# Embedding loads moved ahead of weight loads in a compression stage, and the order of the first weight splits

## The chip, the core and the metric

The kernel runs on one core of one Trainium2 chip. The core has a matrix engine (TensorE, in the profile PE for its matmuls and PEld for its weight loads), a vector engine (DVE), a scalar engine (ACT), GpSimd (POOL) and SyncE (SP). Each engine takes its instructions strictly in program order, and they are synchronised by semaphores. POOL and SP also issue transfers from memory (DMAs). Matrix products are collected in the banks of PSUM, from which ACT and DVE read them.

The metric is the device time of one execution in microseconds (us), and of several executions the median. Less is better.

## The reference

One layer of a decoder: a normalised input `h` goes through one wide projection, whose columns feed sparse attention (with compressed, selected and windowed keys and values), a gated MLP and the merge gates. Then come an output projection, a per-layer embedding and a last normalisation. The sequence has 512 positions, the model 2048 channels. What matters here is the beginning, up to the compression of the keys and values:

```python
h = rms_norm(x, norm_g[l])
proj = h @ w_in[l]
q, kv, g_logits, z_a, uv, z_b, merge_logits = jnp.split(proj, SPLIT_IDX, axis=-1)
k_c, v_c, k_s, v_s, k_w, v_w = [t.reshape(b, s, A_KV_GROUPS, HEAD_DIM)
                                for t in jnp.split(kv, 6, axis=-1)]

def compress(kv, pe, w1, w2):
    b, s, g, d = kv.shape
    ch = kv.reshape(b, s // CMP_STRIDE, CMP_STRIDE, g, d)
    nc = s // CMP_STRIDE - CMP_RATIO + 1
    blocks = jnp.concatenate([ch[:, r:nc + r] for r in range(CMP_RATIO)], axis=2)
    blocks = blocks + pe[None, None, :, None, :]
    hid = jax.nn.silu(jnp.einsum('bnlgd,lde->bnge', blocks, w1))
    return jnp.einsum('bnge,ef->bngf', hid, w2)
```

`compress` is called for keys (`pe_k`, `w1_k`, `w2_k`) and for values (`pe_v`, `w1_v`, `w2_v`). `pe` is the embedding that the title speaks of, 32 x 64 numbers; `w1` and `w2` are the weights.

## The kernel before

**Numbers in two halves.** Matmuls run on 32-bit operands of reduced precision, so each operand is split into a high half (a rounded copy, made by ACT, L99 or L101) and a low half (what the rounding lost, made by DVE, L105 or L107). A product is three matmuls: high by high, and the two mixed ones.

**Jobs, loads and subs.** The projections are a list of jobs, in a generator (`gemm`) that emits matmuls in program order. The first jobs are kc0 and kc1 (the keys to be compressed), then vc0 and vc1 (the values), then the other keys, named k in the profile, and so on. Each covers 128 output columns and all 16 slices of 128 channels (k = 0 to 15). A load brings 8 slices of weights (512 KB) into one of three raw buffers; it is issued on SP's queue (`load_to`, L139). A sub is 4 slices, half a load. Subs 0 to 3 belong to kc0, 4 to 7 to kc1, 8 to 11 to vc0, 12 to 15 to vc1. `split_to(i)` (L144) makes the high halves of all subs up to i + 1 and the low halves of all up to i; when the second sub of a load has its low half, the raw buffer is free and the next load is issued (L171). The halves of kc0 and kc1 are kept in `ob_h` and `ob_l`; later subs go through four `hi` and three `lo` buffers.

**The first two jobs** run in `early()` (L175), in two passes: first the left 256 positions (hf 0) of kc0 and kc1, then the right 256 (hf 1) of both. Every 4 slices `early` calls `split_to`, with `state["ahead"]` added in the first pass. `fill(n)` advances the generator by n steps, a step being one slice, that is three matmuls in these jobs.

**The beginning of the program** (L582 to L662) interleaves them with the input. The four tiles of x (128 positions each) are squared and summed by ACT (`stats`, L603, L604) and scaled by DVE (`scale`, L607, L610). Then PE transposes them (`turn`, L620), and ACT and DVE write them as act_h and act_l (`turned`). Tiles 0 and 1 are handled first, and the first 14 steps of kc0 run between them. Then come 3 steps, `stats` and `scale` of tile 2, 6 steps, `stats` and `scale` of tile 3, and 9 steps; then the transposes of tiles 2 and 3, with the second pass between them. Since ACT and DVE take instructions in order, where a split is emitted decides which work stands ahead of it.

**The compression** (L681 to L718): POOL clears a corner of the tiles `tokk` and `tokv`, and issues ten loads: for k and then for v `w1` (512 KB, L688), and twice in turn `w2` (L692) and the embedding `pe` (L693). `finish("kc1")` (L694) runs the jobs to the end of kc1. Then, for k and v, PE transposes the embedding (L697, into `ps_pe`), and DVE copies it into two places of `tok` (L699, L700). `finish("vc1")` runs vc0 and vc1, and after four more steps `hidden("k")` multiplies `tok` by `w1`. So the transposes stand in PE's order between kc1's last and vc0's first matmul.

Of the kernel before, what the change touches and what calls it, by code (L numbers as in the profile page):

```python
# [20 lines left out]
P = 128  # L21
# [31 lines left out]
def kernel(ctx: ExitStack, tc: tile.TileContext, x, p, norm_g, w_in,  # L53
                      pe_k, w1_k, w2_k, pe_v, w1_v, w2_v, ln_g, ln_b, sgu_w, sgu_b,
                      w_up_a, w_up_b, w_out, w_ple, w_ple_gate, final_g, out):
    nc = tc.nc
    x, out = x[0], out[0]
    p = p[0, 0]
# [10 lines left out]
    def bank(kind, name):  # L69
        return psum.tile([P, 512], F32, tag=kind, name=name)  # L70
# [20 lines left out]
    def flush():  # L91
        todo = list(deferred)
        deferred.clear()
        for f in todo:
            f()

    def high(hi, src, scale=None):
        if scale is None:
            nc.scalar.copy(hi, src)  # L99
        else:  # L100
            nc.scalar.mul(hi, src, scale)  # L101

    def low(hi, lo, src, scale=None):
        if scale is None:
            nc.vector.tensor_tensor(out=lo, in0=src, in1=hi.bitcast(F32), op=ALU.subtract)  # L105
        else:
            nc.vector.scalar_tensor_tensor(out=lo, in0=src, scalar=scale, in1=hi.bitcast(F32),  # L107
                                           op0=ALU.mult, op1=ALU.subtract)
# [10 lines left out]
    jobs, subs, loads = [], [], []  # L119
# [13 lines left out]
    state = {"loads": 0, "high": 0, "low": 0, "ahead": 0, "pops": 2}  # L133
# [7 lines left out]
            raw[state["loads"]] = (t, k0)  # L141
            state["loads"] += 1

    def split_to(i):  # L144
        while state["high"] <= min(i + 1, len(subs) - 1):
            job, k, n, li = subs[state["high"]]
            t, k0 = raw[li]
            if job.keep is not None:
                hi = ob_h[:, job.keep + k // 4].rearrange("p (n c) -> p n c", n=n)
            elif k >= job.kt - job.tail:  # L150
                hi = f_tiles["th"][:, k - job.kt + job.tail:][:, :n]
            else:
                hi = stream.tile([P, n, job.cols], F32R, tag="hi", name="hi", bufs=4)
            src = t[:, k - k0:k - k0 + n]
            high(hi, src)
            parts[state["high"]] = [hi, None, src]
            state["high"] += 1
        while state["low"] <= min(i, len(subs) - 1):
            job, k, n, li = subs[state["low"]]
            pt = parts[state["low"]]  # L160
            if job.keep is not None:
                pt[1] = ob_l[:, job.keep + k // 4].rearrange("p (n c) -> p n c", n=n)
            elif k >= job.kt - job.tail:
                pt[1] = f_tiles["tl"][:, k - job.kt + job.tail:][:, :n]
            else:
                pt[1] = stream.tile([P, n, job.cols], F32R, tag="lo", name="lo")
            low(*pt)
            state["low"] += 1
            li = subs[state["low"] - 1][3]
            if state["low"] == len(subs) or subs[state["low"]][3] != li:  # L170
                load_to(li + 3)  # L171
# [3 lines left out]
    def early():  # L175

        ps = [bank("g", "ps_" + job.name) for job in jobs[:2]]
        for hf in range(2):
            sl = slice(256 * hf, 256 * hf + 256)
            for i, job in enumerate(jobs[:2]):  # L180
                for k in range(job.kt):
                    s = 4 * i + k // 4
                    if k % 4 == 0:
                        flush()
                        split_to(s + state["ahead"] if hf == 0 else 3 + s if i else 7)
                    hi, lo, _ = parts[s]
                    ah, al = job.act(k)
                    st, sp = k == 0, k == job.kt - 1
                    w = k % 4
                    nc.tensor.matmul(ps[i][:, sl], hi[:, w], ah[:, sl], start=st, stop=False)  # L190
                    nc.tensor.matmul(ps[i][:, sl], hi[:, w], al[:, sl], start=False, stop=False)
                    nc.tensor.matmul(ps[i][:, sl], lo[:, w], ah[:, sl], start=False, stop=sp)
                    if not sp:
                        yield
                if hf:
                    flush()
                    job.evac(ps[i])
                    done.add(job.name)
                yield
# [60 lines left out]
    def fill(n):  # L260
        for _ in range(n):
            next(run, None)

    def finish(name):
        while name not in done:
            next(run)
        flush()
# [314 lines left out]
    with tc.tile_pool(name="xin", bufs=4, side="right") as xin:  # L582
        xt = [xin.tile([P, D], F32, tag="xt", name=f"xt{t}") for t in range(TT)]
        g_row = xin.tile([KT, P], F32, name="g_row", bufs=1)
        g_col = xin.tile([P, KT], F32, name="g_col", bufs=1)
        st = xin.tile([P, TT, 2], F32, name="st", bufs=1)
        nc.sync.dma_start(g_row, norm_g.rearrange("(k p) -> k p", p=P))
        for t in range(TT):
            nc.sync.dma_start(xt[t], x[t * P:t * P + P])
            if t == 1:  # L590
                load_to(1)
        load_to(2)

        spin = bank("g", "ps_spin")

        def keep_busy(n):

            for _ in range(n):
                nc.tensor.matmul(spin[:, :P], ident, ident, start=True, stop=True)

        def stats(t):
            sq = xin.tile([P, D], BF16, tag="sq", name="sq", bufs=1)
            nc.scalar.activation(sq, xt[t], AF.Square, accum_out=st[:, t, 0:1])  # L603
            nc.scalar.activation(st[:, t, 1:2], st[:, t, 0:1], AF.Sqrt, bias=eps_t, scale=1.0 / D)  # L604

        def scale(t):
            nc.vector.reciprocal(st[:, t, 0:1], st[:, t, 1:2])  # L607
            for c in range(0, D, D if t % 2 == 0 else D // 2):
                sl = slice(c, c + (D if t % 2 == 0 else D // 2))
                nc.vector.tensor_scalar(out=xt[t][:, sl], in0=xt[t][:, sl], scalar1=st[:, t, 0:1], scalar2=None,  # L610
                                        op0=ALU.mult)

        banks = {}

        def turn(hf, kp):

            b = banks[hf, kp] = bank("ststoo"[len(banks) % 6], "ps_x")
            for j in range(4):
                k, t = 2 * kp + j // 2, 2 * hf + j % 2
                nc.tensor.transpose(b[:, j * P:j * P + P], xt[t][:, k * P:k * P + P], ident)  # L620

        def turned(hf, kp):
            sl = slice(2 * hf * P, 2 * hf * P + 2 * P)
            for j in range(2):
                k = 2 * kp + j
                split(act_h[:, k, sl], act_l[:, k, sl], banks[hf, kp][:, 2 * P * j:2 * P * (j + 1)],
                      g_col[:, k:k + 1], later=True)
            flush()

        keep_busy(10)  # L630
        b = bank("o", "ps_g")
        nc.tensor.transpose(b[:, :KT], g_row, ident[:KT, :KT])
        nc.vector.tensor_copy(g_col, b[:, :KT])
        keep_busy(22)
        for t in range(2):
            stats(t)
            scale(t)
        split_to(0)
        pairs = KT // 2
        for kp in range(4):  # L640
            turn(0, kp)
        for kp in range(pairs):
            turned(0, kp)
            if kp + 4 < pairs:
                turn(0, kp + 4)
            if kp:
                fill(2)
        state["ahead"] = 1
        for t, n in ((2, 3), (3, 6)):
            fill(n)  # L650
            stats(t)
            scale(t)
        fill(9)
        for kp in range(4):
            turn(1, kp)
        for kp in range(pairs):
            turned(1, kp)
            if kp + 4 < pairs:
                turn(1, kp + 4)
            if kp:  # L660
                fill(2)
        state["ahead"] = 2  # L662
# [18 lines left out]
    with tc.tile_pool(name="cmp", bufs=1) as cmp:  # L681
        w1t, w2t, pet = {}, {}, {}
# [2 lines left out]
            nc.gpsimd.memset(tok[n][:, :, :, NCMP:], 0.0)  # L685
        for n, w1, w2, pe in (("k", w1_k, w2_k, pe_k), ("v", w1_v, w2_v, pe_v)):
            w1t[n] = cmp.tile([P, 16, HD], F32, name="w1" + n)
            nc.gpsimd.dma_start(w1t[n], w1.rearrange("l d e -> (l d) e").rearrange("(m p) e -> p m e", p=P))  # L688
            w2t[n] = cmp.tile([HD, 2, HD], F32, name="w2" + n)
            pet[n] = cmp.tile([NCMP, 2, HD], F32, name="pe" + n)  # L690
            for i in range(2):
                nc.gpsimd.dma_start(w2t[n][:, i], w2)  # L692
                nc.gpsimd.dma_start(pet[n][:, i], pe)  # L693
        finish("kc1")  # L694
        for n in "kv":
            b = bank("t", "ps_pe")
            nc.tensor.transpose(b[:, :NCMP], pet[n].rearrange("l i d -> l (i d)"), ident[:NCMP, :NCMP])  # L697
# [236 lines left out]
    n = len(slots)  # L934
# [142 lines left out]
    for cg in range(4):  # L1077
# [10 lines left out]
        for j in range(4):  # L1088
# [4 lines left out]
            h, l = x2_act(k)  # L1093
# [31 lines left out]
```

## Time and profile before

| | us |
|---|---|
| median of 3 runs | 1671.33 |
| lowest and highest run | 1670.41, 1671.61 |
| profiled execution, its own time | 1672.25 |
| span of its trace | 1670.5 |
| PE busy in the span | 1648.9 |
| ACT busy, DVE busy | 617.9, 736.9 |
| POOL busy | 107.8 |
| mean granted clock of TensorE | 0.996 |

The profile is one execution, seen by the hardware profiler. A row of its timeline reads: start, duration, engine, line of the kernel, operation, output and inputs, their shapes, count, and in brackets how long the engine had stood idle and what it waited for. A matmul's duration contains its fill and drain; matmuls overlap, so that the distance between two starts is what one costs. The granted clock is 1 at full speed.

### The profile page before, as it was taken

Reading aid. Unit: us, or ns where it says so; the run is one execution under the profiler, and the core shown is the slowest. Engines: PE = TensorE matmul, PEld = TensorE weight load, DVE = VectorE, ACT = ScalarE, POOL = GpSimd, SP = SyncE. Lnnn points to the kernel's source line nnn. Section 1 sums busy time; section 2 is a strip of 40 time slices with the busy share of each in tenths; the row PEclk is TensorE's granted clock in tenths of the full one; section 3 lists DMA queues with packets and bytes.
Section 4 is the critical chain, followed back from the end, with each engine's and each line's share of the span. In section 5 each row is a group of like instructions: output and inputs, shape, how many; then the busy total and the mean of one; then the engine's idle time right before and its main releaser. Section 6 shows DMA issues by size and latency. Waiting matters only on the chain.

```text
span 1670.5 us, 20864 instructions
## 1 busy us (share of the span) xinstructions
PE 1648.9 (99%) x7981; PEld 1381.6 (83%) x7981; DVE 736.9 (44%) x1487; ACT 617.9 (37%) x1253; POOL 107.8 (6%) x136
## 2 busy tenths in 40 slices
PE   8899999999999999999999999999999999999997
PEld 8779888888888888888888888888888888888886
DVE  6243378988873352343222222332235333333335
ACT  7232356766653322332222222222224222223334
POOL 1000001110110011000000000000000000001100
PEclk9999999999999999999999999999999999999999
DMA  5322421112234333344333333333334433333333
GB/s 191 102 63 79 114 59 52 51 39 51 51 98 117 101 88 89 89 101 113 95 95 101 96 94 101 89 100 101 91 99 155 139 98 88 91 124 91 99 101 126
DMA packets 214482, 159.64 MB, mean 96 GB/s; under 512 B 4832, under 2 KB 190320, under 8 KB 212848
## 3 DMA queue, kind: packets, MB, share of 16 engines
q1 hardware_dynamic: 212976, 151.41, 32.5%
q0 software_dynamic: 1408, 6.92, 1.2%
q8 instruction: 62, 1.02, 0.3%
q14 instruction: 36, 0.29, 0.1%
HBM read 154.12 MB, written 4.19 MB: 95 GB/s over the span
## 4 chain that ended last, share of the span: by engine, by line
PE 93%; DVE 2%; ACT 1%; DMA 0%; issue 0%; DVEq 0%; ACTq 0%
PE ps_wo L230 3%; PE ps_wo L232 3%; PE ps_wo L231 3%; PE ps_mb L223 3%; PE ps_ma L224 3%; PE ps_mb L224 3%; PE ps_ma L223 3%; PE ps_ma L222 3%; PE ps_mb L222 3%; PE ps_pg L231 3%; PE ps_pg L232 3%; PE ps_pg L230 3%; PE ps_za L222 2%; PE ps_t L822 2%; PE ps_za L224 2%; PE ps_za L223 2%
## 5 line engine op out<-in xcount | busy, mean ns | idle before, releaser
L105 DVE TENSOR_TENSOR lo<-raw,hi 128x512 fp32r<-128x512 f32 (+1 forms) x528 | 361.7, 688 | 652.7 <-PE ps_mb L224 127.4
L99 ACT CAST hi<-raw 128x512 fp32r<-128x512 f32 (+1 forms) x528 | 323.5, 615 | 731.6 <-PE ps_wo L232 102.5
L230 PE MATMUL ps_wo<-hi,act_h 128*128 128x512 f32 x256 | 101.0, 395 | 0.0
L232 PE MATMUL ps_wo<-hi,act_l 128*128 128x512 f32 x256 | 99.9, 390 | 0.0
L231 PE MATMUL ps_wo<-lo,act_h 128*128 128x512 f32 x256 | 99.8, 390 | 0.0
L224 PE MATMUL ps_ma<-act_h,lo 128*128 128x512 f32 x256 | 99.7, 389 | 0.0
L223 PE MATMUL ps_mb<-act_l,hi 128*128 128x512 f32 x256 | 99.7, 389 | 0.0
L223 PE MATMUL ps_ma<-act_l,hi 128*128 128x512 f32 x256 | 99.7, 389 | 0.0
L222 PE MATMUL ps_ma<-act_h,hi 128*128 128x512 f32 x256 | 99.7, 389 | 0.0
L224 PE MATMUL ps_mb<-act_h,lo 128*128 128x512 f32 x256 | 99.7, 389 | 0.0
L222 PE MATMUL ps_mb<-act_h,hi 128*128 128x512 f32 x256 | 99.7, 389 | 0.0
L783 ACT ACTIVATE prob<-prob,st 128x512 f32<-128x512 f32 (+3 forms) x128 | 70.7, 555 | 4.2 <-DVE st L774 4.1
L99 ACT CAST pth<-ps_t 128x512 fp32r<-128x512 f32 (+1 forms) x88 | 47.9, 544 | 65.6 <-PE ps_t L822 65.2
L105 DVE TENSOR_TENSOR ptl<-ps_t,pth 128x512 fp32r<-128x512 f32 (+1 forms) x88 | 56.3, 640 | 21.1 <-ACT pth L99 20.2
L774 DVE CUSTOM_DVE_ANT_0 prob<-ps_s,b 128x512 f32<-128x512 f32 (+3 forms) x128 | 56.3, 487 | 9.8 <-PE ps_s L771 9.6
L465 POOL TENSOR_TENSOR m<-sig,sig 128x512 f32<-128x512 f32 x16 | 27.1, 1693 | 493.6 <-DVE sig L463 493.6
L232 PEld LDWEIGHTS ps_wo<-hi,act_l 128*128 128x128 f32 x256 | 48.1, 188 | 10.3
L222 PEld LDWEIGHTS ps_mb<-act_h,hi 128*128 128x128 f32 x256 | 48.1, 188 | 10.0
L223 PEld LDWEIGHTS ps_ma<-act_l,hi 128*128 128x128 f32 x256 | 48.1, 188 | 10.0
L222 PEld LDWEIGHTS ps_ma<-act_h,hi 128*128 128x128 f32 x256 | 48.1, 188 | 10.0
L223 PEld LDWEIGHTS ps_mb<-act_l,hi 128*128 128x128 f32 x256 | 48.1, 188 | 10.0
L224 PEld LDWEIGHTS ps_ma<-act_h,lo 128*128 128x128 f32 x256 | 48.1, 188 | 9.9
(314 smaller groups left out, 3726.8 us busy)
## 6 DMA issues: line engine op xcount, KB each, us to landing
raw<-in_w_in_dram SPq DMA_DIRECT2D x164, 512.0 KB, 3.7
raw<-in_w_out_dram SPq DMA_DIRECT2D x32, 512.0 KB, 3.6
raw<-in_w_ple_gate_dram SPq DMA_DIRECT2D x32, 512.0 KB, 3.6
raw<-in_w_up_a_dram SPq DMA_DIRECT2D x16, 512.0 KB, 3.7
raw<-in_w_up_b_dram SPq DMA_DIRECT2D x16, 512.0 KB, 3.8
xt<-in_x_dram SPq DMA_DIRECT2D x4, 1024.0 KB, 7.7
m<-in_x_dram POOLq DMA_DIRECT2D x4, 1024.0 KB, 8.0
out_dram<-m SPq DMA_DIRECT2D x3, 1024.0 KB, 3.8
```

The lines of the kernel that those rows point to most:

```text
L99: nc.scalar.copy(hi, src)
L105: nc.vector.tensor_tensor(out=lo, in0=src, in1=hi.bitcast(F32), op=ALU.subtract)
L222: nc.tensor.matmul(ps, hi[:, j], ah, start=st, stop=False)
L223: nc.tensor.matmul(ps, hi[:, j], al, start=False, stop=False)
L224: nc.tensor.matmul(ps, lo[:, j], ah, start=False, stop=sp)
L230: nc.tensor.matmul(o, ah[:, sl], hi[:, j], start=st, stop=False)
L231: nc.tensor.matmul(o, ah[:, sl], lo[:, j], start=False, stop=False)
L232: nc.tensor.matmul(o, al[:, sl], hi[:, j], start=False, stop=sp)
L465: nc.gpsimd.tensor_tensor(out=merge_tiles["m"][:, f], in0=merge_tiles[0], in1=t, op=ALU.add)
L774: nc.vector.tensor_tensor_reduce(out=pt[:, j * n:j * n + n], in0=o[:, j], in1=b0[:, 512 - n:], scale=-SLOPE[h], scalar=3.0e38, op0=ALU.add ...
L783: nc.scalar.activation(sl, sl, AF.Exp, bias=st[:, 0, j, hh:hh + 1], scale=-1.0, accum_out=st[:, 1, j, hh:hh + 1])
L822: nc.tensor.transpose(b[:, (2 * e + hh) * P:(2 * e + hh + 1) * P], pts[hh][:, c:c + P], ident)
```

## The change

Three things are edited.

The first is in the compression. For each of k and v both copies of the embedding are loaded ahead of `w1`, and `w2` after it. So POOL's order of loads becomes pe, pe, w1, w2, w2 for k and then the same for v. The tiles are allocated as before.

The second is where the embeddings are transposed: `finish("vc0")` stands in place of `finish("kc1")`, so that the transposes and their copies come in program order between vc0 and vc1.

The third is in the beginning. `split_to` gets a second argument, `more`: the number of subs by which the high halves run ahead of the low ones (1 before, and when it is not given). After the first 14 steps the subs 4 and 5 are split, then `stats` and `scale` of tile 2 follow, then subs 6 and 7, then `stats` and `scale` of tile 3, and only then 18 steps at once. `early` no longer adds `state["ahead"]`, and at sub 7 makes no high half ahead. So the high half of sub 8 is made at the first step of the second pass, and that of sub 9 within kc1's second pass.

```diff
-    def split_to(i):
-        while state["high"] <= min(i + 1, len(subs) - 1):
+    def split_to(i, more=1):
+        while state["high"] <= min(i + more, len(subs) - 1):
...
                     if k % 4 == 0:
                         flush()
-                        split_to(s + state["ahead"] if hf == 0 else 3 + s if i else 7)
+                        split_to(s if hf == 0 else 3 + s if i else 7, 0 if s == 7 else 1)
...
-        state["ahead"] = 1
-        for t, n in ((2, 3), (3, 6)):
-            fill(n)
-            stats(t)
-            scale(t)
-        fill(9)
+        split_to(5, 0)
+        stats(2)
+        scale(2)
+        split_to(7, 0)
+        stats(3)
+        scale(3)
+        fill(18)
         for kp in range(4):
             turn(1, kp)
...
             w1t[n] = cmp.tile([P, 16, HD], F32, name="w1" + n)
-            nc.gpsimd.dma_start(w1t[n], w1.rearrange("l d e -> (l d) e").rearrange("(m p) e -> p m e", p=P))
             w2t[n] = cmp.tile([HD, 2, HD], F32, name="w2" + n)
             pet[n] = cmp.tile([NCMP, 2, HD], F32, name="pe" + n)
             for i in range(2):
+                nc.gpsimd.dma_start(pet[n][:, i], pe)
+            nc.gpsimd.dma_start(w1t[n], w1.rearrange("l d e -> (l d) e").rearrange("(m p) e -> p m e", p=P))
+            for i in range(2):
                 nc.gpsimd.dma_start(w2t[n][:, i], w2)
-                nc.gpsimd.dma_start(pet[n][:, i], pe)
-        finish("kc1")
+        finish("vc0")
```

## The prediction

> **What bounds the kernel now.** I read the page first. TensorE (PE) is busy for all but 21.6 us of the span, so only time in which it waits, or runs at a lower clock, can be won. The two rows of tenths cut the span in 40 slices: PE has gaps in the first two and in the last, and no slice has a granted clock below nine tenths on average. All numbers are microseconds of this one profiled execution.
>
> ```profile
> span 1670.5 us, 20864 instructions
> PE 1648.9 (99%) x7981; PEld 1381.6 (83%) x7981; DVE 736.9 (44%) x1487; ACT 617.9 (37%) x1253; POOL 107.8 (6%) x136
> ...
> PE   8899999999999999999999999999999999999997
> ...
> PEclk9999999999999999999999999999999999999999
> ```
>
> The list of PE's waits over the whole span says which ones are left. Each row is the waiting group, what it waited for, the total, the number of times and the longest.
>
> ```profile
> PE ps_pe L697 <- DMA pev<-in_cmp_pe_v_dram: 3.8, 1, 3.8
> PE ps_kc L192 <- DVE ob_l L105: 2.1, 3, 1.2
> ```
>
> The first is one wait: the transpose of v's embedding (L697), placed after job kc1, waits for the embedding's load. The second is PE in the first two jobs waiting for the low half of a weight split. The timeline of PE (start, duration) shows what surrounds the first.
>
> ```profile
> 45.20 0.28 PE L190 MATMUL ps_kc<-act_h,ob_h 128*128 128x256 f32 x1
> ...
> 45.44 0.28 PE L192 MATMUL ps_kc<-act_h,ob_l 128*128 128x256 f32 x1
> 46.11 0.21 PE L697 MATMUL ps_pe<-ident,pek 32*128 32x32 f32 x1 [0.39 <-PE ps_kc L192]
> 50.17 0.31 PE L697 MATMUL ps_pe<-ident,pev 32*128 32x32 f32 x1 [3.85 <-DMA pev<-in_cmp_pe_v_dram]
> 50.41 0.80 PE L222 MATMUL ps_vc<-act_h,hi 128*128 128x512 f32 x1
> ...
> 55.70 0.53 PE L222 MATMUL ps_vc<-act_h,hi 128*128 128x512 f32 x1
> 56.06 0.39 PE L223 MATMUL ps_vc<-act_l,hi 128*128 128x512 f32 x1
> ...
> 64.02 0.39 PE L222 MATMUL ps_vc<-act_h,hi 128*128 128x512 f32 x1
> ```
>
> Job kc1 issues its last matmul at 45.44 and vc0 its first at 50.41. The 14th of vc0's 48 matmuls starts at 56.06, the first of vc1 (the 49th) at 64.02: (64.02 - 56.06) / 35 = 0.227 a matmul at full speed. The 13 before 56.06 took 5.65, or 0.43 each. The table of stretches (PE, PEld, DVE, ACT and POOL busy, then the granted clock) gives the reason: a clock of 0.50 after the wait.
>
> ```profile
> 50.17:55.70 5.53, 5.53 (x14) 4.31 (x15) 0.35 (x2) 0.19 (x1) 0.00 (x0) 0.50 0.01 3
> ```
>
> So the late load costs twice, the wait and then half speed.
>
> **Part 1, the embeddings: what goes.** POOL issues the ten loads of the compression one after another.
>
> ```profile
> 38.62 0.16 POOL L685 MEMSET tokk<- 128x64 f32 x1 [35.07 <-DVE act_l L107]
> ...
> 39.19 1.34 POOL L688 DMA_DIRECT2D w1k<-in_cmp_w_k_dram  x1 [0.33 <-issue]
> ...
> 44.32 0.52 POOL L693 DMA_DIRECT2D pev<-in_cmp_pe_v_dram  x1
> ...
> 45.96 0.50 POOL L693 DMA_DIRECT2D pev<-in_cmp_pe_v_dram  x1
> ```
>
> v's second embedding copy is the tenth, issued at 45.96, after PE wanted it. The same ten loads remain. In the new order it is seventh: before it stand w1k (1.34) and five small ones, 0.52 each by the rows here, 3.9 in all. It is issued at 39.19 + 3.9 = 43.1, or earlier by what the queue itself starts earlier: the queue waits for the last act_l. The transposes move behind vc0, which by the sum below ends about 54.8.
>
> ```profile
> w1v<-in_cmp_w_v_dram POOLq DMA_DIRECT2D x1, 512.0 KB, 6.8
> ...
> pev<-in_cmp_pe_v_dram POOLq DMA_DIRECT2D x2, 8.0 KB, 4.8
> ```
>
> From issue to landing these loads take 4.8, the slowest on this queue 6.8. So pev lands between 47.9 and 49.9, 4.9 to 6.9 before it is wanted. The wait is gone, and PE goes from kc1 straight to vc0. vc0's splits are ready: they are made while kc1's second half runs (part 2). What the wait cost: kc1's next slot was 45.44 + 0.12 = 45.56. At 0.227, vc0 would have had to start at 56.06 - 13 x 0.227 = 53.10 to be where it was. Difference **7.54**: 4.85 of wait (with the two transposes) and 2.69 of half clock.
>
> The clock's part is the less certain. The row has 5.5 at half clock. The Trainium skill (TensorE: Matmul & The Clock Gate, Part 1, the HAM clock gate) says that a window of about 3.4 us without activity halves the clock and a busy window of the same length, at a free-running phase, restores it. An estimate from that page is 3.4 at half speed and 1.7 lost, against the row's 2.69; by it part 1 would be 6.5 instead of 7.5, varying from run to run. The trace agrees that the drop follows a stretch with hardly a matmul (45.7 to 50.2).
>
> **What comes in its place.** Two transposes and four small DVE copies between vc0 and vc1. Nearest rows for the transposes: eight others between matmuls of 512 columns; for the copies, one of the four before.
>
> ```profile
> 50.59 0.17 DVE L699 COPY tokv<-ps_pe 64x16 f32<-64x16 f32 x1 [2.82 <-PE ps_pe L697]
> ...
> 500.06 0.40 PE L232 MATMUL ps_vn<-hi,act_l 128*128 128x512 f32 x1
> 500.30 1.04 PE L991 MATMUL ps_w<-ident,ws 128*128 128x128 f32 x8
> 501.09 0.48 PE L230 MATMUL ps_vn<-hi,act_h 128*128 128x512 f32 x1
> 501.40 0.39 PE L231 MATMUL ps_vn<-lo,act_h 128*128 128x512 f32 x1
> ```
>
> From the free slot (500.06 + 0.23) to where the stream is back in step (501.40 - 0.23): 0.88 for eight, 0.22 for two. Upper bound: if the 0.55 between 45.56 and 46.11 was the switch itself and not k's load, 0.55 + 0.24 + 0.1 = 0.9. I take **0.3**, near the lower row, since pek's second copy was also landing about 46. The copies lie on DVE ahead of vc1's third split, which PE wants after two splits of twelve matmuls, 5.4 later; uncovered they would cost 4 x 0.17 = 0.7.
>
> **Part 2, the first jobs' splits.** ACT before (L99 makes high halves, L603 the squares), DVE (L105 low halves, L610 the scaling), SP's queue and PE, in order of time:
>
> ```profile
> 19.52 1.25 ACT L99 CAST ob_h<-raw 128x512 fp32r<-128x512 f32 x2
> ...
> 21.36 0.62 ACT L99 CAST ob_h<-raw 128x512 fp32r<-128x512 f32 x1 [0.59 <-DMA raw<-in_w_in_dram]
> ...
> 21.87 0.37 SPq L139 DMA_DIRECT2D raw<-in_w_in_dram  x1
> 21.89 1.91 ACT L603 ACTIVATE sq<-xt 128x2048 bf16<-128x2048 f32 x1
> ...
> 24.62 1.91 ACT L603 ACTIVATE sq<-xt 128x2048 bf16<-128x2048 f32 x1
> ...
> 25.64 0.68 DVE L105 TENSOR_TENSOR ob_l<-raw,ob_h 128x512 fp32r<-128x512 f32 x1
> ...
> 26.04 0.28 PE L190 MATMUL ps_kc<-act_h,ob_h 128*128 128x256 f32 x1
> ...
> 26.86 1.13 ACT L99 CAST hi<-raw 128x512 fp32r<-128x512 f32 x2
> ...
> 27.18 1.42 DVE L610 TENSOR_SCALAR xt<-xt,st 128x1024 f32<-128x1024 f32 x2
> 28.51 0.69 DVE L105 TENSOR_TENSOR ob_l<-raw,ob_h 128x512 fp32r<-128x512 f32 x1
> ...
> 29.25 0.39 PE L192 MATMUL ps_kc<-act_h,ob_l 128*128 128x256 f32 x1 [1.18 <-DVE ob_l L105]
> ...
> 30.56 2.78 PE L620 MATMUL ps_x<-ident,xt 128*128 128x128 f32 x24
> 31.19 5.94 ACT L101 ACTIVATE act_h<-ps_x,g_col 128x256 fp32r<-128x256 f32 x16 [3.21 <-PE ps_x L620]
> 32.06 6.36 DVE L107 SCALAR_TENSOR_TENSOR act_l<-ps_x,g_col,act_h 128x256 fp32r<-128x256 f32 x16 [2.26 <-PE ps_x L620]
> ```
>
> Low half 7 stands on DVE behind the scaling of the fourth x tile and comes at 28.51; PE wants it before 28 and waits 1.18. The new order on ACT is highs 4, 5, squares of tile 2, highs 6, 7, squares of tile 3. High 6 no longer makes the squares wait: they start at 19.52 + 1.25 = 20.8 instead of 21.89, highs 6 and 7 run at about 23.0 to 24.1, and the squares of tile 3 at 24.0 instead of 24.62. On DVE the scaling of tile 2 ends at about 24.5, lows 6 and 7 at 25.1 and 25.8, and the scaling of tile 3 at 28.6 - 0.6 = 28.0. Both low halves are there before PE wants them (26.3 and 27.7). The eight steps of kc1 from 26.04 then last 8 x 0.36 = 2.88 (a step is three matmuls, 45.44 + 0.12 - 45.20 = 0.36), and PE reaches its transposes at 28.92 instead of 30.56: **1.64** gained. They want tile 3 at about 29.0, 1.0 after it is scaled: that is late next, and nothing is paid unless ACT slips by more. The gain lies between 0.6 (tile 3 later by all of that) and 1.64.
>
> High 8 moves between the fourth and fifth of the sixteen act_h. ACT is then 0.6 later for the other twelve. DVE, which starts 0.87 after ACT and is slower (6.36 against 5.94), takes most of that up; PE wants the last low half at (45.20 - 15 x 0.36 + 0.12) - 0.37 = 39.55 before the shift, and DVE ended at 38.42: 1.1 of cover against at most 0.6. High 8's raw tile was issued at 21.87 and used at 26.86 before without a wait, so at 31 it doesn't wait; queued behind it are the act_h, and PE behind these. Highs 9 and 10 and lows 8 to 10 come under kc1's second half, 16 x 0.36 = 5.8 long; they take about 1.3 on ACT and 2.1 on DVE. The load that low 7 releases on SP's queue goes out 2.8 earlier, the one behind low 9 about 1 earlier; none of the raw loads is wanted sooner than 10 after issue there. Cost taken: 0; uncovered at most 0.6.
>
> **Sum.** 7.54 + 1.64 - 0.3 = 8.9 faster. The profiled execution took 1672.25 (its span and 1.75 around it): 1663.4. It lies 0.92 above the median of the three runs, 1671.33, from which the sum gives 1662.4. I forecast 1662.9, between the two, since the half-clock stretch, which I price from this execution, may have been shorter in the faster runs. PE is saturated behind 64 up to the last 10 us, so nothing later takes it back.
>
> **Rivals.** *The reorder gives nothing* (R1): ACT's chain slips and PE waits for tile 3 or for an act_l behind high 8 instead. For it, ACT's and DVE's rows leave hardly a gap there; against it, the slack of 1.0 and the removed 0.59 wait. Gain 7.2: 1664.6. *The half clock comes anyway* (R2), because something other than the wait lowers it. For it: the two are seen together only once. Against it: a second such stretch would show as a slice under nine tenths only if it were longer, but PE has no other wait of its length. Gain 6.2: 1665.6. *The wait only moves* (R3, the slower side): pev's landing, now behind w1k's 512 KB, comes after vc0. It begins to cost from 54.8; with the half clock of 2.69 behind it, it decides from a wait of 6.2, a landing at 61.0, 18 after issue. At 63 the time would be 1673. Against it stands every landing on that queue, 6.8 at most. Where the transposes wait in step with w1k only, there is no loss at all.
>
> **How the numbers follow.** Forecast 0.79, R1 0.10, R2 0.06, R3 0.03, and 0.02 for a late pev that takes back most of the gain. About 0.2%, 3.3 us, is what a measurement of this kernel can tell from no change, so the forecast, R1 and R2 are all faster: 0.95; same 0.02; slower 0.03. The range goes from 1661.0 (the lowest run shown, 1670.41, less 9.2, with the transposes free, rounded down) to 1666.5 (R2 at the profile's own time, 1666.1, and the transposes at their upper bound in part).
>
> **What would show it.** Right: no row of PE waiting for pev; a clock of 1.0 from 40 to 60; vc0's first matmul at about 43.9 and vc1's at 55.2; L697 between them with under 1 us; L192's waits down from 2.1 to about 0.9 (the longest goes); transposes L620 at about 28.9. Wrong: a wait of L620 for xt, of L190 or L191 for act_h or act_l around 33, of L697 for a load, or any stretch under full clock.

## The result and the profile after

The changed kernel takes 1663.42 us (median of 5 runs, 1663.36 to 1663.46), the kernel before 1671.33 (median of 5, 1670.41 to 1671.61). The ratio is 0.9954, with a 95% interval from 0.9939 to 0.9968. That is 7.9 faster, beyond the 0.2% that a measurement can tell from no change, and within the range that was forecast; the forecast was 1662.9. The profiled execution took 1663.46 with a span of 1661.8, so the spans differ by 8.7, against 8.9 in the sum.

From the page of the changed kernel, the same rows as before:

```profile
span 1661.8 us, 20864 instructions
PE 1645.4 (99%) x7981; PEld 1378.3 (83%) x7981; DVE 737.4 (44%) x1487; ACT 617.8 (37%) x1253; POOL 107.7 (6%) x136
...
PE   9999999999999999999999999999999999999997
...
PEclk9999999999999999999999999999999999999999
```

The same number of instructions runs on every engine. The first two slices of PE have gone from 8 to 9, and PE is busy 3.5 less in sum, although its work is the same; the half speed, which made 2.7 of it, is gone. Its list of waits over the whole span, where pev stood first:

```profile
PE ps_spin L599 <- POOL eps_t L75: 1.4, 1, 1.4
PE ps_x L620 <- DVE xt L610: 1.4, 1, 1.4
PE ps_t L824 <- DVE ptl L105: 1.2, 1, 1.2
PE ps_kc L192 <- DVE ob_l L105: 1.0, 2, 0.5
```

No embedding is in it any more (the transposes are now L699), and L192 waits twice instead of three times. The waits for `ps_spin`, `ps_x` and `ps_t` were there before too. PE's timeline around the old place and the new one:

```profile
43.80 0.28 PE L192 MATMUL ps_kc<-act_h,ob_l 128*128 128x256 f32 x1
43.92 0.40 PE L222 MATMUL ps_vc<-act_h,hi 128*128 128x512 f32 x1
...
54.60 0.39 PE L224 MATMUL ps_vc<-act_h,lo 128*128 128x512 f32 x1
54.92 0.24 PE L699 MATMUL ps_pe<-ident,pek 32*128 32x32 f32 x1
55.00 0.22 PE L699 MATMUL ps_pe<-ident,pev 32*128 32x32 f32 x1
55.15 0.50 PE L222 MATMUL ps_vc<-act_h,hi 128*128 128x512 f32 x1
55.49 0.39 PE L223 MATMUL ps_vc<-act_l,hi 128*128 128x512 f32 x1
```

vc0 starts 0.12 after kc1's last matmul, and vc1 at 55.15 instead of 64.02. The stretch that ran at half clock before, in the table of stretches (columns as before), now has 1.00:

```profile
50.17:55.70 5.53, 5.53 (x26) 4.33 (x25) 0.86 (x2) 1.29 (x3) 0.00 (x0) 1.00 0.36 105
```

POOL's timeline, with the new order of loads:

```profile
37.40 0.16 POOL L686 MEMSET tokk<- 128x64 f32 x1 [33.84 <-DVE act_l L107]
...
37.97 1.21 POOL L692 DMA_DIRECT2D pek<-in_cmp_pe_k_dram  x2 [0.33 <-issue]
39.16 1.22 POOL L693 DMA_DIRECT2D w1k<-in_cmp_w_k_dram  x1
...
41.40 1.03 POOL L692 DMA_DIRECT2D pev<-in_cmp_pe_v_dram  x2
```

pev's second copy goes out at 41.9, and the list of DMA issues gives the time from issue to landing:

```profile
pev<-in_cmp_pe_v_dram POOLq DMA_DIRECT2D x2, 8.0 KB, 5.1
```

So it is there at 47.0, eight before PE wants it. And the beginning of the program, on ACT, DVE and PE in order of time:

```profile
20.55 2.03 ACT L603 ACTIVATE sq<-xt 128x2048 bf16<-128x2048 f32 x1
...
22.91 1.13 ACT L99 CAST ob_h<-raw 128x512 fp32r<-128x512 f32 x2
23.95 1.90 ACT L603 ACTIVATE sq<-xt 128x2048 bf16<-128x2048 f32 x1
24.44 1.29 DVE L105 TENSOR_TENSOR ob_l<-raw,ob_h 128x512 fp32r<-128x512 f32 x2
...
26.50 1.42 DVE L610 TENSOR_SCALAR xt<-xt,st 128x1024 f32<-128x1024 f32 x2
...
28.92 2.78 PE L620 MATMUL ps_x<-ident,xt 128*128 128x128 f32 x24
...
31.00 0.64 ACT L99 CAST hi<-raw 128x512 fp32r<-128x512 f32 x1
...
32.41 4.79 DVE L107 SCALAR_TENSOR_TENSOR act_l<-ps_x,g_col,act_h 128x256 fp32r<-128x256 f32 x12 [0.32 <-ACT act_h L101]
```

Low halves 6 and 7 are done at 24.44 + 1.29 = 25.7, tile 3 is scaled at 27.9, and PE's transposes start at 28.92. High half 8 stands at 31.00 among the act_h and makes DVE wait 0.32, of which nothing reaches PE.

### The profile page after: what moved, and what is told of

Read it like the earlier page. It is cut to its first block, busy times and chain, and to the rows that moved or that the text cites. A ratio compares the mean times of both kernels' runs of the same rounds, so it can differ in the third digit from the quotient of the medians.

```text
span 1661.8 us, 20864 instructions
## 1 busy us (share of the span) xinstructions
PE 1645.4 (99%) x7981; PEld 1378.3 (83%) x7981; DVE 737.4 (44%) x1487; ACT 617.8 (37%) x1253; POOL 107.7 (6%) x136
## 4 chain that ended last, share of the span: by engine, by line
PE 95%; DVE 3%; ACT 1%; DMA 0%; issue 0%; SPq 0%; DVEq 0%; ACTq 0%
PE ps_wo L230 4%; PE ps_wo L232 4%; PE ps_wo L231 4%; PE ps_ma L223 3%; PE ps_mb L223 3%; PE ps_mb L222 3%; PE ps_ma L222 3%; PE ps_mb L224 3%; PE ps_ma L224 3%; PE ps_pg L230 3%; PE ps_pg L231 3%; PE ps_pg L232 3%; PE ps_za L222 2%; PE ps_za L224 2%; PE ps_t L824 2%; PE ps_za L223 2%
## 5 line engine op out<-in xcount | busy, mean ns | idle before, releaser
L224 PEld LDWEIGHTS ps_mb<-act_h,lo 128*128 128x128 f32 x256 | 48.0, 188 | 10.0
```

The costliest lines, as they stand in the source:

```text
L224: nc.tensor.matmul(ps, lo[:, j], ah, start=False, stop=sp)
```

## The experiments

The theory at this point: the place of the transposes removes the wait and the half clock; the order of the loads does nothing further; the splits add their 1.6 only because the wait is gone. Rivals: the order of the loads is what counts, or the two parts simply add, or the half clock has nothing to do with the wait. The kernel before was timed beside every group of runs; its medians there were 1670.74 (21 runs, the first four experiments), 1671.63 (15, beside the kernels with 36 matmuls in the wait and with low halves two and four steps earlier) and 1670.76 (21, beside the other three). Its single runs fall into two groups: 27 of the 57 lie at 1670.2 to 1671.0 (median 1670.65), the other 30 at 1671.2 to 1672.4 (median 1671.69). The mean granted clock is 0.997 in 23 of the first and 0.996 in all of the second.

### The embeddings alone

```diff
-        finish("kc1")
+        finish("vc0")
```

together with the new order of loads; the splits stay as before.

> Only the two edits to the embeddings: loads first, transposes behind vc0; the splits are as before. If the parts add up (my theory): PE goes from kc1 to vc0 without a wait, clock 1.0 throughout; vc0's first matmul at 45.6 (kc1's end of before); the low-half waits of L192 stay at 2.1 in sum. Time 1663.42 + 1.64 = 1665.1, and runs as close together as the changed kernel's (0.1), since no half-clock stretch is left. Rival, the splits are what frees vc0: a wait at vc0's first matmul stays, 1666 or more.

Measured: 1664.97 (1664.76 to 1665.24); ratio to before 0.9964 (0.9950 to 0.9978). PE's timeline:

```profile
45.33 0.28 PE L192 MATMUL ps_kc<-act_h,ob_l 128*128 128x256 f32 x1
45.45 0.40 PE L222 MATMUL ps_vc<-act_h,hi 128*128 128x512 f32 x1
```

PE goes straight on at the old end of kc1, at full speed. The theory's number was 1665.1. The runs spread 0.5, somewhat more than expected.

### The splits alone

The edits to `split_to`, `early` and the beginning; loads and place as before.

> Only the edits to the first splits; the embeddings load and are transposed as before. Theory: PE reaches the transposes 1.64 earlier, but the wait for pev ends when POOL's queue delivers it, and that starts only 1.2 earlier (37.4 instead of 38.6 in the two traces). So the wait grows by 0.4 to about 4.2, the half clock behind it stays, and the gain is about 1.2: 1670.1. Rival, the parts add: 1.64, 1669.7. The times can hardly tell these two apart (before's runs spread over 1.2); the trace can: second L697 at 48.9 to 49.0 (theory) or 48.5 (rival).

Measured: 1670.38 (1669.62 to 1670.96); ratio 0.9995 (0.9986 to 1.0004), no difference that can be told. PE's timeline:

```profile
44.78 0.22 PE L698 MATMUL ps_pe<-ident,pek 32*128 32x32 f32 x1 [0.73 <-DMA pek<-in_cmp_pe_k_dram]
48.69 0.24 PE L698 MATMUL ps_pe<-ident,pev 32*128 32x32 f32 x1 [3.70 <-DMA pev<-in_cmp_pe_v_dram]
48.87 0.80 PE L222 MATMUL ps_vc<-act_h,hi 128*128 128x512 f32 x1
```

L192's long wait is gone as in the changed kernel, and PE arrives early at the transposes, only to wait for k's embedding too (0.73). Both waits end when the loads land: pev at 48.7, between the two numbers expected, 1.5 earlier than before, mostly because POOL began 1.25 earlier. So in this execution vc0 starts at 48.87 instead of 50.41, and nearly all of the 1.64 gets through the wait. The median can't show it: its interval reaches from 2.3 faster to 0.7 slower, and the half clock differs from run to run (by the granted clock it lasted from 48.8 to 52.2 here, from 49.2 to 56.0 in the profiled execution of before). With the embeddings moved, the same edit is worth 1664.97 - 1663.42 = 1.55.

### The old order of loads in the changed kernel

```diff
-                nc.gpsimd.dma_start(pet[n][:, i], pe)
-            nc.gpsimd.dma_start(w1t[n], ...)
-            for i in range(2):
+            nc.gpsimd.dma_start(w1t[n], ...)
+            for i in range(2):
                 nc.gpsimd.dma_start(w2t[n][:, i], w2)
+                nc.gpsimd.dma_start(pet[n][:, i], pe)
```

> The changed kernel with the loads in the order of before (w1, then w2 and pe in turns); the transposes stay behind vc0. Theory: pev's last copy is issued at about 44.7 and lands by 50, PE wants it at 54.9, so the place alone removes the wait and the order of the loads is worth nothing: 1663.4, within 0.2, no L697 wait. Rival, the order of the loads is needed: a wait at L697 and up to 1667.

Measured: 1663.50 (1663.41 to 1663.60), the changed kernel's time. POOL's timeline shows pev's second copy as the last load, at 44.38:

```profile
44.38 0.50 POOL L694 DMA_DIRECT2D pev<-in_cmp_pe_v_dram  x1
```

and PE's shows its transpose in its place, without a wait:

```profile
55.04 0.22 PE L698 MATMUL ps_pe<-ident,pev 32*128 32x32 f32 x1
```

The order of the loads, which the change's name puts first, is worth nothing once the transposes stand behind vc0.

### The old place in the changed kernel

```diff
-        finish("vc0")
+        finish("kc1")
```

> The changed kernel with the transposes back between kc1 and vc0; the loads stay in the new order. Theory: pev's last copy is issued at 41.9 and lands at about 47.0, PE wants it at 44.2: a wait of about 2.8 to 3.1. That is shorter than the 4.5 idle of before. If the clock falls only after an idle stretch longer than about 3.4 (the Trainium skill, TensorE: Matmul & The Clock Gate, Part 1), it stays at 1.0 and the time is 1663.4 + 3.0 - 0.3 = 1666.2. If any wait of that kind halves it, up to 2.7 more: 1667 to 1669, with runs that spread.

Measured: 1668.00 (11 runs, 1666.22 to 1669.42); ratio to before 0.9983 (0.9975 to 0.9992). So the order of loads and the splits without the move bring 2.7; against the splits alone (1670.38) the order is worth 2.4 in the old place. PE's timeline:

```profile
43.84 0.28 PE L192 MATMUL ps_kc<-act_h,ob_l 128*128 128x256 f32 x1
44.05 0.24 PE L699 MATMUL ps_pe<-ident,pek 32*128 32x32 f32 x1
47.05 0.21 PE L699 MATMUL ps_pe<-ident,pev 32*128 32x32 f32 x1 [2.76 <-DMA pev<-in_cmp_pe_v_dram]
47.20 0.59 PE L222 MATMUL ps_vc<-act_h,hi 128*128 128x512 f32 x1
47.59 0.63 PE L223 MATMUL ps_vc<-act_l,hi 128*128 128x512 f32 x1
...
50.57 0.54 PE L224 MATMUL ps_vc<-act_h,lo 128*128 128x512 f32 x1
```

The wait was as expected (2.76), the clock not: matmuls of 0.63 follow it up to 50.6. The runs lie in three groups: one at 1666.2 (the time expected with a full clock), six at 1667.85 to 1668.0 and four at 1669.0 to 1669.4. The mean granted clock is 0.998 in the first and 0.996 or 0.997 in the ten others. So a wait of 2.8 halves the clock in nearly every run, for a stretch that differs from run to run.

### The wait filled with work

The kernel before, with matmuls of the identity in the place where PE waits (their result is not used):

```diff
         finish("kc1")
+        wb = bank("o", "ps_warm")
+        for _ in range(36):
+            nc.tensor.matmul(wb[:, :P], ident, ident, start=True, stop=True)
```

> The kernel before, with 36 matmuls of the identity (128 columns, result unused) between kc1's last matmul and the transposes, where PE waits for pev; nothing else is changed. It leaves the wait as it is and fills it with activity. Theory (the half clock comes from the idle stretch alone): second L697 still at about 50.2, clock 1.0 from 40 to 60, no matmul of 0.63 behind it, and 1663.42 + (4.85 - 0.3) + 1.64 = 1669.6 with runs within 0.3 of each other, where before's 21 runs lie between 1670.3 and 1672.2. Rival (the half clock comes anyway, R2 of the prediction): the stretch at 0.50 stays, 1670.7, and the runs spread as before's.

Measured: 1672.87 (1672.68 to 1673.35), slower than either theory had it. PE's timeline gives the reason:

```profile
45.17 8.20 PE L697 MATMUL ps_warm<-ident 128*128 128x128 f32 x72
53.30 0.24 PE L700 MATMUL ps_pe<-ident,pek 32*128 32x32 f32 x1
```

Each of the 36 ran as two, and together they outlasted the wait by some 3. In the table of stretches the clock nevertheless was full:

```profile
40.00:60.00 20.00, 20.00 (x147) 18.74 (x146) 4.93 (x12) 3.51 (x8) 5.48 (x10) 1.00 0.41 103
```

That speaks for the theory, but the time was mis-sized, so it was repeated with 18.

> The kernel before with 18 matmuls of the identity in the wait instead of 36. In the run with 36 each ran as two of 0.114, 8.1 in all, and outlasted the wait; 18 take 4.1 and end at about 49.7, before pev lands at about 50. Theory (the half clock comes from the idle stretch): clock 1.0 from 40 to 60, vc0's first matmul at 50.3, time 1663.42 + 4.55 + 1.64 = 1669.6 (or 1672.87 of the run with 36, less the 3.2 by which its matmuls outlasted pev's landing: 1669.7), runs within 0.3. Rival (the half clock comes anyway): 1671 to 1672, spread over 1 or more.

Measured: 1669.50 (1668.95 to 1670.08). PE's timeline:

```profile
45.24 4.18 PE L697 MATMUL ps_warm<-ident 128*128 128x128 f32 x36
...
49.92 0.24 PE L700 MATMUL ps_pe<-ident,pev 32*128 32x32 f32 x1 [0.32 <-DMA pev<-in_cmp_pe_v_dram]
50.09 0.50 PE L222 MATMUL ps_vc<-act_h,hi 128*128 128x512 f32 x1
50.42 0.40 PE L223 MATMUL ps_vc<-act_l,hi 128*128 128x512 f32 x1
```

pev lands about as late as before and vc0 starts about as late, but at full speed (0.40 instead of 0.63). The time is the theory's 1669.6. The runs spread over 1.1 and not 0.3, though the mean granted clock is 0.998 in all eleven; what spreads them isn't shown. The half clock comes from the idle stretch, and what it costs in the median is 1670.76 - 1669.50 = 1.3, half of the 2.69 in the one execution that the prediction was made from.

With 10, some 2 of idle time are left:

> The same with 10: 2.3 of activity from 45.5 to 47.8, then idle until pev lands at 50, 2.2. Theory A (the clock falls when a stretch near the page's window of 3.4 passes almost idle; 3.0 was enough in the kernel with the old place): 2.2 is too short, clock 1.0, 1669.6 as with 18. Theory B (any stall of two or more halves it): a stretch at 0.50 behind it and 1670.3 to 1672, runs spread.

Measured: 1670.59, in two groups: four runs at 1668.95 to 1669.53, seven at 1670.52 to 1670.80, with a mean granted clock of 0.998 in the first and 0.997 in the second. The profiled one (1670.8) is of the second:

```profile
49.86 0.24 PE L700 MATMUL ps_pe<-ident,pev 32*128 32x32 f32 x1 [1.97 <-DMA pev<-in_cmp_pe_v_dram]
50.04 0.50 PE L222 MATMUL ps_vc<-act_h,hi 128*128 128x512 f32 x1
```

The table of stretches has the clock before and after its fall:

```profile
48.03:51.44 3.41, 1.58 (x7) 1.32 (x8) 0.67 (x4) 0.00 (x0) 0.00 (x0) 1.00 0.06 16
51.44:54.86 3.42, 3.42 (x10) 2.63 (x9) 0.46 (x1) 0.62 (x1) 0.00 (x0) 0.50 0.00 0
```

Theory A falls for most runs: an idle stretch of 2.0 was enough. And the clock fell only at about 51.4, when PE had been at work again for 1.4, and came back 3.4 later. In the traces of the splits alone and of the old place it came back 3.4 after its fall as well (48.8 to 52.2, 47.5 to 50.9). In before's it took twice that:

```profile
49.15:52.57 3.42, 2.40 (x6) 1.95 (x7) 0.35 (x2) 0.00 (x0) 0.00 (x0) 0.50 0.02 5
52.57:55.98 3.41, 3.41 (x9) 2.64 (x9) 0.04 (x1) 0.47 (x1) 0.00 (x0) 0.50 0.00 0
```

There the clock fell while PE still waited, and the first 3.4 at half clock had PE busy for 2.4 only. All this fits a decision taken every 3.4 over the stretch that went before, which some runs meet and some don't; the decision itself is in no trace.

### The two waits that are left in the beginning

In the changed kernel L192 still waits 1.0 for low halves 2 and 3. Two kernels emit them earlier, so that on DVE they stand ahead of act_l that they stood behind: by two steps

```diff
+                    elif k % 4 == 2 and hf == 0 and s < 3:
+                        split_to(s + 1, 0)
```

> The changed kernel, with low halves 1 to 3 of kc0 emitted two steps earlier, so that on DVE each stands ahead of two act_l that it stood behind. Theory: the two waits of L192 that are left (0.47 and 0.48, at 19.7 and 21.9) go, PE reaches the transposes L620 at 28.2 instead of 28.9, and tile 3 is scaled at 27.9, just before: 1663.4 - 0.7 = 1662.7. Rival (DVE is the bound there, so that the act_l come later by what the low halves come earlier): L191 waits instead, 1663.4 or up to 0.5 above.

and by four.

```diff
-                        split_to(s if hf == 0 else ...
+                        split_to(min(s + 1, 3) if hf == 0 and i == 0 else s if hf == 0 else ...
```

> As the kernel with low halves two steps earlier, but four steps earlier. DVE's total work up to low half 5 is the same. Theory: the end of kc0's first pass is set by the last act_l, so there is no more to gain than with two steps: 1662.7, within 0.2. Rival: the earlier high halves make ACT wait for raw tiles or delay act_h, 1663.4 or more.

Two steps: 1662.61 (1662.61 to 1662.74), 0.8 under the changed kernel; one of the two waits goes, one stays:

```profile
PE ps_kc L194 <- DVE ob_l L105: 0.5, 1, 0.5
```

Four steps: 1663.64 (1663.49 to 1663.85), nothing gained. The edit also moved the high halves, and ACT's timeline shows that one of them was emitted ahead of its load:

```profile
19.31 0.62 ACT L99 CAST ob_h<-raw 128x512 fp32r<-128x512 f32 x1 [1.08 <-DMA raw<-in_w_in_dram]
```

So the low halves alone were moved by four steps:

```diff
-                        ... 0 if s == 7 else 1)
+                        ... 0 if s == 7 or (hf == 0 and i == 0 and s) else 1)
```

> The kernel with low halves four steps earlier, but with the high halves left where the changed kernel has them, so that ACT doesn't wait for the raw tile of high half 4 (1.08 in that run). Theory (that wait was the loss): no wait of ACT for raw at 19, L191 waits at most 0.2, 1662.4 to 1662.7. Rival (four steps are too early whatever the high halves do, since act_l comes late): 1663.4 or more.

Measured: 1662.61 (1662.54 to 1662.65). PE's timeline:

```profile
20.64 0.39 PE L191 MATMUL ps_kc<-act_l,ob_h 128*128 128x256 f32 x1 [0.38 <-DVE act_l L107]
...
28.02 2.78 PE L620 MATMUL ps_x<-ident,xt 128*128 128x128 f32 x24
```

PE no longer waits for a low half, but for an act_l (0.38, more than expected), and reaches the transposes at 28.02, about as with two steps (28.09). Both kernels, at 1662.61, beat the kernel before and the changed one, and gain the same. The raw tile that ACT waited for was what the other lost by: without that wait the same low halves are 1.0 faster.

## Why the prediction was right, and where it was off

**The wait is gone, and the transposes cost little: right.** vc0's first matmul was forecast for 43.9 and vc1's for 55.2; they came at 43.92 and 55.15. The detour of the two transposes is 55.49 - 0.23 - (54.60 + 0.23) = 0.43, against 0.3 taken and bounds of 0.2 and 0.9.

**Why it is gone: half right.** The prediction credited the new order of loads and the new place together. With the splits in, the place alone does it (1663.50 with the old loads), and the order alone, in the old place, leaves a wait of 2.76 and a half clock in most runs. The slower rival R3, a pev that lands after vc0, didn't come about: landing at 47.0, pev had eight to spare, and even as the last load it came in time. The bound of 6.8 that the prediction set against R3 was misread. It holds for the first 60 us; over the whole span the list of DMA issues has a slower load on POOL's queue:

```profile
m<-in_x_dram POOLq DMA_DIRECT2D x4, 1024.0 KB, 8.0
```

These bring 1024 KB each. With 8.0, pev would have been due by 43.1 + 8.0 = 51.1 at the latest, still ahead of 54.8.

**The half clock: right in its cause, too large for the median.** R2 is refuted: with the wait filled the clock stays full, with the place restored it falls. For the execution that the term of 2.69 came from, the sum holds: 1672.25 - 8.9 = 1663.35, and 1663.42 was measured. But that execution is among the slowest of before. Against the kernel with 18 matmuls (1669.50) the two groups of before's runs, with medians of 1670.65 and 1671.69, lie 1.1 and 2.2 higher. So the term was 0.5 to 1.6 too large, depending on the group. The forecast, which lay half way between the sum taken off the median (1662.4) and off the profiled execution (1663.4), made up for half of that and came out 0.5 too low. With 1.1 or 2.2 for the half clock, and 0.43 for the transposes, the sum is 7.2 or 8.3, and taken off its group's median either gives 1663.4. How near the measured gain of 7.9 came is thus in part luck: three of the five runs of before that stood beside the result are of the upper group; against the 21 runs with a median of 1670.74 the gain is 7.3.

The Trainium skill (TensorE: Matmul & The Clock Gate, Part 1, the HAM clock gate) says that the window that decides is free-running, so that where the clock changes varies. The traces agree: the clock fell 1.0 before the wait ended in before's, and 1.4 after vc0 had begun in the one with 10 matmuls. The prediction's estimate from that page, 1.7, is nearer to the median's 1.3 than the profile's row was, and it is the distance between the profiled run in the old place (1667.96) and the one run there at full clock (1666.22). The advice of the Trainium skill to leave no idle gap of more than about 3 (same page, Why this matters for your kernels) is too generous here: a gap of 2.0 cost some 1.5 in seven runs of eleven.

**The splits: right, by their own steps.** Squares of tile 2 at 20.8 (20.55 came), of tile 3 at 24.0 (23.95), low half 7 at 25.8 (25.7), tile 3 scaled at 28.0 (27.9), transposes at 28.92 (28.92). The cover of 1.0 held, and R1 didn't come about. High half 8 cost PE nothing. A side remark was off: the load that low half 7 releases goes out at 25.76 instead of 29.27, 3.5 earlier and not 2.8, since 28.51 is where that half begins and not where it is done; no term hung on it. What the sum didn't say is that the 1.64 depends on part 1: alone the same edit gave 0.4 in the median, which can't be told from nothing. In its one trace the wait let 1.5 of the 1.64 through, because the queue that ends the wait had itself begun earlier, so it is the varying half clock, more than the wait, that hides the gain there.

## What to carry to other kernels

When a load is late, move its consumer behind work that is ready anyway before reordering the queue: here the move did all of it, and the order, worth 2.4 in the old place, added nothing behind it. A gain in front of a wait counts only as far as what ends the wait comes earlier too. And where a stall drops the clock, don't take its price from one execution: look at how the runs group, and price the stall with and without.

## What the runs showed of the hardware

An idle stretch of 2.0 halved TensorE's clock in seven runs of eleven, going by the mean granted clock (0.997 instead of 0.998), one of 2.8 in ten of eleven, one of 0.3 in none of eleven. In the four profiled executions that show the fall, PE had been busy for 0.1, 0.2, 0.7 and 1.6 of the 3.4 ahead of it. The fall can come 1.4 after work has resumed. The clock came back 3.4 after its fall in three of them, and 6.8 after it in before's, where PE was busy for only 2.4 of the first 3.4.

The changed kernel, without such a stretch, has runs within 0.1 of each other, where those of before lie up to 2.1 apart.
